# Attention in four placed chains behind the GLU, low passes first, ten weight buffers through the down projection, and ScalarE rows for the SSM's angles and decay

## The chip, the cores and the metric

The kernel runs on one core of a Trainium2 chip. The metric is the device time of one execution in microseconds (us), as the median of three runs. The engines named below are TensorE (PE in the profile, PEld for its weight loads), VectorE (DVE), ScalarE (ACT) and SyncE (SP, which issues the DMAs). The compiled program fixes an order of instructions on each engine; each engine then works through its own list in that order and stops at an instruction whose input or buffer is not there yet.

## The reference

One decoder block on 256 tokens of width 2048. The columns of one input projection feed a state-space model (SSM) with a gate (GLU) and a sparse attention; both halves go through one output projection, a normalisation, and a feed-forward part with a width-3 convolution.

```python
proj = h @ w_in[l]
u_ssm, q, k, v, qi, ki, wi = jnp.split(proj, split_at, axis=-1)
y_ssm = _s5_mixer(u_ssm, ...)      # a decaying, turning state per channel; then
                                   # y = gelu(y);  y * sigmoid(y @ w_glu + b_glu)
y_attn = _dsa_attention(q, k, v, qi, ki, wi * idx_w_scale)
                                   # relu(qi . ki), weighted sum over 16 index heads, causal,
                                   # the 64 best keys of each query, softmax with a slope per head
mix = jnp.concatenate([y_ssm, y_attn], axis=-1) @ w_out[l]
h = _layer_norm(DEEPNORM_ALPHA * h + mix, ln1_g[l], ln1_b[l])
f = (gelu(conv(h @ w_up)) * (h @ w_gate)) @ w_down      # 5632 wide, 44 tiles of 128
h = _layer_norm(DEEPNORM_ALPHA * h + f, ln2_g[l], ln2_b[l])
```

## The kernel before

All matrix products are made from a high and a low part of each operand: `mm3` issues three matmuls (high by high, low by high, high by low) for one product of 128 rows.

**Weights.** A table of sources (`order`) is cut into halves of 128x1024 numbers. `fetch` brings one half by DMA into a raw tile (SP), makes its high part on ACT (`wh`, L133) and its low part on DVE (`wl`, L136). `next_half` keeps `state["ahead"]` halves made in advance, four as a rule. Extra buffers for some halves come from the table `special`, at times and places where another tile's memory is free.

**Input projections** (`acc`, L186 to L188). The projections for the SSM, the index queries, keys, values and two groups of four query heads (`q0`, `q1`) run one after another, 16 products each. `pump` lets a background job issue a few instructions after each product. The SSM is such a job, in four rounds (`ssm_in`): each round makes angles (`angles`, L362), sines and cosines, the decay rows (L547) and a scan on DVE. Another is the indexer: matmuls (L655), `rel` on ACT (L661), weighted sums `score` on DVE (L666), eight rounds of taking and striking out the eight best (L671, L672), and a mask `nm` for each block `b` of 128 queries (L675).

**GLU and attention.** `glu_in` makes Gelu of the SSM's output and splits it. `attention(c)` does for one key head `c` block 0 and then block 1 of the queries: scores on PE (L720), mask added on DVE (L724), maximum (L726), four Exp on ACT, a reciprocal and four scalings on DVE (L734), transposes on PE (L740), a copy `pt` on ACT (L743), products with the values (L747) and a split into `mix`. It is a generator: each `yield` waits for the next `pump`. `attention(0)` is pumped beside the products of the GLU, `attention(1)` beside those of the output projection. `in_turn` ties each function that needs a table of ACT (Sin, Gelu, Exp, Sigmoid) behind the last such one in the order in which the program is written, so the Sigmoid of the first GLU tile is written behind the Exp of `attention(0)`.

**Output projection, feed-forward.** The output projection accumulates in column groups `db` of 512, units of two products (`rows_half`), for 128 tokens each. The feed-forward's up and gate products go tile by tile through `wide_half`, which issues eight high passes (512 columns) and eight low passes (256 columns) for each half `kh` of the 2048 rows; in the second half one high pass is put last. The down projection (`e`) takes two halves for each of 44 tiles `f`; its last five tiles (`LAG`) are run for 128 tokens first and for the other 128 afterwards, so that ten halves must be held at once, and `state["ahead"]` is raised from four to ten at `f` = 34.

## Time and profile before

| what | us |
|---|---|
| median of three runs | 1144.31 |
| the three runs | 1144.85, 1138.44, 1144.31 |
| the profiled execution, its time | 1139.62 |
| the profiled execution, its span | 1137.8 |
| PE busy in the span | 1097.6 (96%) |
| DVE busy | 748.2 (66%) |
| ACT busy | 563.7 (50%) |
| DMA, mean over the span | 180 GB/s |

The rows further down are of the profiled execution; times in them count from the start of its span, which is 1.8 us shorter than its time. A row's bracket, where it has one, gives the engine's idle time before it and what ended that. PEclk is the clock that TensorE was granted: 1.00 and 0.50 stand for 2.4 and 1.2 GHz.

### The profile page before, as it was taken

What the parts mean: (1) busy time and instruction counts of PE and PEld (TensorE: products, weight loads), DVE (VectorE), ACT (ScalarE), POOL (GpSimd) and SP (SyncE); (2) the same over time, 40 slices, a digit from 0 to 9 for tenths busy, and PEclk for the clock granted to TensorE, in tenths of its full rate; (3) what the DMA queues carried; (4) which work ended last, traced back from release to release, by engine and by line L of the source; (5) the groups of instructions that cost most, each with busy time, mean ns of one, the idle gap of its engine ahead of it and who ended that gap; (6) DMA issues with size and microseconds to landing.
All of it is one profiled execution on the core that took longest, in us unless ns stands there. A gap on an engine that the chain in (4) does not pass through costs nothing.

```text
span 1137.8 us, 16797 instructions
## 1 busy us (share of the span) xinstructions
PE 1097.6 (96%) x6576; PEld 945.3 (83%) x6576; DVE 748.2 (66%) x1052; ACT 563.7 (50%) x813; POOL 0.2 (0%) x4
## 2 busy tenths in 40 slices
PE   8999999877999999999999999999999999999975
PEld 7998999767878888888888888888888888888864
DVE  7979998785666756677666565666565544444557
ACT  5865436445554755555444555545555444444430
POOL 0000000000000000000000000000000000000000
PEclk9999999988999999999999999999999999999988
DMA  8753444323566375555755555555554655555632
GB/s 267 237 167 115 159 145 145 139 74 108 207 212 214 104 259 192 185 185 187 262 194 190 189 189 187 192 187 187 185 188 165 216 189 186 186 188 190 212 130 74
DMA packets 59310, 204.44 MB, mean 180 GB/s; under 512 B 7264, under 2 KB 10080, under 8 KB 58592
## 3 DMA queue, kind: packets, MB, share of 16 engines
q1 hardware_dynamic: 59232, 203.38, 52.8%
q8 instruction: 51, 0.84, 0.3%
q14 instruction: 27, 0.22, 0.1%
HBM read 200.20 MB, written 2.10 MB: 178 GB/s over the span
## 4 chain that ended last, share of the span: by engine, by line
PE 86%; DMA 6%; DVE 3%; ACT 2%; issue 1%; SPq 1%; DVEq 0%; ACTq 0%
PE pd L206 41%; PE e L186 6%; PE e L188 6%; PE e L187 6%; PE acc L188 4%; PE acc L186 4%; PE acc L187 4%; DMA raw<-in_w_down_dram 3%; PE o L188 3%; PE o L187 3%; PE o L186 3%; DMA raw<-in_w_in_dram 1%; PE misc L599 1%; PE bu L556 1%; DVE wl L136 1%
## 5 line engine op out<-in xcount | busy, mean ns | idle before, releaser
L136 DVE TENSOR_TENSOR wl<-raw,wh 128x1024 fp32r<-128x1024 f32 x333 | 406.8, 1223 | 309.9 <-ACT wh L133 308.5
L133 ACT ACTIVATE wh<-raw 128x1024 fp32r<-128x1024 f32 x333 | 352.1, 1058 | 339.4 <-PE pd L206 141.5
L206 PE MATMUL pd<-mix,wh 128*128 128x512 f32 x1344 | 337.7, 393 | 0.7 <-ACT gate L1005 0.7
L206 PEld LDWEIGHTS pd<-mix,wh 128*128 128x128 f32 x1344 | 241.5, 189 | 44.0 <-ACT gate L1005 1.1
L206 PEld LDWEIGHTS pd<-mix,wl 128*128 128x128 f32 x1344 | 183.3, 190 | 13.1
L206 PE MATMUL pd<-mix,wl 128*128 128x256 f32 x1344 | 187.4, 282 | 0.0
L186 PE MATMUL e<-wh,acth 128*128 128x512 f32 x304 | 120.6, 397 | 5.5 <-ACT wh L133 5.5
L187 PE MATMUL e<-wh,actl 128*128 128x512 f32 x304 | 120.3, 396 | 0.0
L188 PE MATMUL e<-wl,acth 128*128 128x512 f32 x304 | 119.6, 396 | 0.5 <-DVE wl L136 0.5
L186 PE MATMUL acc<-x,wh 128*128 128x256 f32 (+1 forms) x400 | 113.9, 285 | 1.4 <-ACT x L181 1.2
L187 PE MATMUL acc<-x,wl 128*128 128x256 f32 (+1 forms) x400 | 114.2, 286 | 0.7 <-DVE wl L136 0.5
L188 PE MATMUL acc<-x,wh 128*128 128x256 f32 (+1 forms) x400 | 114.1, 285 | 0.8 <-DVE x L182 0.8
L186 PEld LDWEIGHTS acc<-x,wh 128*128 128x128 f32 (+1 forms) x400 | 75.8, 190 | 3.1 <-ACT x L181 1.4
L187 PEld LDWEIGHTS acc<-x,wl 128*128 128x128 f32 (+1 forms) x400 | 75.8, 190 | 2.2 <-DVE wl L136 0.7
L188 PEld LDWEIGHTS acc<-x,wh 128*128 128x128 f32 (+1 forms) x400 | 75.9, 190 | 2.1 <-DVE x L182 1.0
L186 PEld LDWEIGHTS e<-wh,acth 128*128 128x128 f32 x304 | 57.1, 188 | 20.0 <-ACT wh L133 6.2
L188 PEld LDWEIGHTS e<-wl,acth 128*128 128x128 f32 x304 | 57.1, 188 | 15.0 <-DVE wl L136 1.0
L187 PEld LDWEIGHTS e<-wh,actl 128*128 128x128 f32 x304 | 57.1, 188 | 13.8
L175 ACT ACTIVATE hc<-hc 128x256 f32<-128x256 f32 x44 | 18.4, 417 | 69.8 <-DVE hc L1046 69.8
L1033 DVE TENSOR_TENSOR sum<-sum,pd 128x256 f32<-128x256 f32 x84 | 34.9, 415 | 0.0
L188 PE MATMUL o<-wl,mix 128*128 128x512 f32 x80 | 31.9, 398 | 0.0
L186 PE MATMUL o<-wh,mix 128*128 128x512 f32 x80 | 31.6, 397 | 0.0
(262 smaller groups left out, 1201.7 us busy)
## 6 DMA issues: line engine op xcount, KB each, us to landing
raw<-in_w_gate_dram SPq DMA_DIRECT2D x88, 512.0 KB, 4.1
raw<-in_w_up_dram SPq DMA_DIRECT2D x88, 512.0 KB, 4.1
raw<-in_w_down_dram SPq DMA_DIRECT2D x88, 512.0 KB, 3.7
raw<-in_w_in_dram SPq DMA_DIRECT2D x51, 512.0 KB, 4.1
raw<-in_w_out_dram SPq DMA_DIRECT2D x32, 512.0 KB, 4.6
raw<-in_w_glu_dram SPq DMA_DIRECT2D x8, 512.0 KB, 3.8
raw<-in_w_v_dram SPq DMA_DIRECT2D x4, 512.0 KB, 4.5
z<-in_x_n_dram SPq DMA_DIRECT2D x1, 2048.0 KB, 8.8
```

Of the source, the lines that this page charges most:

```text
L133: A.activation(h[:, :w], raw[:, :w], AF.Copy)
L136: V.tensor_sub(l[:, :w], raw[:, :w], h[:, :w].bitcast(F32))
L175: ins = A.activation(*args, **kw)
L186: T.matmul(out, lhsT=lh[0], rhs=rh[0], start=start, stop=False)
L187: T.matmul(out, lhsT=lh[1], rhs=rh[0], start=False, stop=False)
L188: return T.matmul(out, lhsT=lh[0], rhs=rh[1], start=False, stop=stop).ins
L206: ins = T.matmul(out[:, 0] if low else out, lhsT=w, rhs=r, start=kh == 0 and i == 0, stop=kh == 1 and i == 15)
L556: T.matmul(bu[:, sd, ri, k:k + 128], lhsT=bt[r, 2 * bi + c_, h, ri, :], rhs=ustk[r, c_, h, :], start=True, stop=True)
L599: T.matmul(yp[32 * q:32 * q + 32, c_, e, k1:], lhsT=cbd[k1 * 2 + ri][:, ct * 4 + q, :], rhs=hv[ri][:, q % 2, k:k + 128 - k1], start=False, ...
L1033: V.tensor_tensor(t, t, p[:, 0], op=ALU.add)
```

## The change

1. **Angles and decay rows.** The one DVE product of 128x1024 in `angles` and the one for `dec` become eight ACT products of 128x128 each (a copy with a scale from a column), in each of the four rounds of the SSM.
2. **Attention.** `attention(c)` becomes a class `Attend` with four steps (scores, weights, turn, values) and one object for each key head and block: `a00`, `a10` (block 0), `a01`, `a11` (block 1). The scores of `a00` and `a10` are issued behind GLU tiles 3 and 4, their weights behind the whole GLU; everything else is issued at numbered units of the output projection, and the order written there is kept by hand on PE.
3. **GLU.** It runs without a background job; its first two tiles are interleaved, six products of each, then the last two of each.
4. **Output projection.** Three column groups are accumulated at once, over the SSM's half of the rows first and the attention's afterwards; the order of its weights, the extra buffers and the reading ahead of ten follow that order.
5. **Low passes first.** In the second half of `wide_half` the eight low passes come ahead of the eight high ones.
6. **Down projection.** Extra buffers for the last 80 halves instead of the last 20, and `ahead` is ten from `f` = 4 on. The split activations of tiles 1 to 43 move into the memory of two `hl` tiles, four to a slot, used in turn.

```diff
-    order += [w_out_d[i] for i in (0, 1, 4, 5, 2, 3, 6, 7, 8, 9, 10, 11, 12, 13, 14, 15)]
+    order += [w_out_d[i] for i in (0, 1, 4, 5, 8, 9, 2, 6, 10, 3, 7, 11, 12, 13, 14, 15)]
...
-        steps = list(passes(0)) + list(passes(1))
-        if kh:
-            steps.append(steps.pop(7))
+        steps = list(passes(1)) + list(passes(0)) if kh else list(passes(0)) + list(passes(1))
...
+    def by_pair(out, a, bi, row):
+
+        for s_ in range(2):
+            for ch in range(4):
+                i = bi * 8 + ch * 2 + s_
+                A.activation(out[:, s_, ch * 128:(ch + 1) * 128], row, AF.Copy, scale=a[:, i:i + 1])
...
-        V.tensor_tensor(v4(c), by_pair(f2, bi), row(cc("iota")), op=ALU.mult)
+        by_pair(c, f2, bi, cc("iota"))
...
-        V.tensor_tensor(v4(dec), by_pair(r2, bi), row(cc("after0")), op=ALU.mult)
+        by_pair(dec, r2, bi, cc("after0"))
...
-    def beside_q():
-        yield from glu_in()
-        yield from attention(0)
-
-    add_bg(beside_q(), 1)
+    a00, a10, a01, a11 = (Attend(c, b) for b in range(2) for c in range(2))
...
+    add_bg(glu_in(), 1)
     qt += proj_four("q1")
     drain()
...
+    first_glu = [(glu_acc(nt), next_half()) for nt in range(2)]
+    for some in (range(6), range(6, 8)):
+        for acc, half in first_glu:
+            glu_products(acc, half, some)
+    for nt in range(8):
...
+        in_turn(sgm, acc[:, :S], AF.Sigmoid, bias=pc("bglu", nt))
+        V.tensor_tensor(sgm, sgm, yt[nt], op=ALU.mult)
+        split(h[:, nt % 4, :], l[:, nt % 4, :], sgm)
+        if nt == 3:
+            a00.scores()
+        if nt == 4:
+            a10.scores()
...
-    add_bg(attention(1), 2)
...
-    for db, some in ((0, range(4)), (1, range(4)), (0, range(4, 8)), (1, range(4, 8)), (2, range(8))):
...
+    a00.weights()
+    a10.weights()
+    beside = {2: a01.scores, 3: a01.weights, 6: a00.turn, 7: a10.turn, 9: a00.values, 10: a10.values,
+              11: a11.scores, 12: a11.weights, 14: a01.turn, 17: a01.values, 22: a11.turn, 25: a11.values}
+    unit = 0
+    with tc.manual_schedule(engines={mybir.EngineType.PE}):
+        for some in (range(4), range(4, 6), range(6, 8)):
...
+            for db in range(3):
+                for i in some:
+                    half = next_half()
+                    for b in range(2):
+                        beside.get(unit, lambda: None)()
+                        rows_half(oacc[db][b], mix, 2 * i, half, b, 16)
+                        unit += 1
...
-    for i in range(4 * LAG):
+    for i in range(16 * LAG):
         if i % (2 * LAG) < 2 * LAG - 4:
-            special[len(halves) - 4 * LAG + i] = spare2(i % (2 * LAG))
+            special[len(halves) - 16 * LAG + i] = spare2(i % (2 * LAG))
...
-        if f == NF - 2 * LAG:
+        if f == NF - 8 * LAG:
             state["ahead"] = 2 * LAG
```

Three places show what this does to the order on the engines.

On ACT, at the start of the input projections, before (L317 brings the SSM's input `u` out of PSUM, L590 makes a diagonal, L366 and L175 make the cosines):

```order
L133 ACTIVATE wh<-raw 128x1024
L317 ACTIVATE u_308<-acc 128x128x2
L133 ACTIVATE wh<-raw 128x1024
L590 ACTIVATE dd<-cst,prm 128x128
L317 ACTIVATE u_342<-acc 128x128x2
L133 ACTIVATE wh<-raw 128x1024
L317 ACTIVATE u_374<-bu 128x128x2
L133 ACTIVATE wh<-raw 128x1024
```

The same place now:

```order
L133 ACTIVATE wh<-raw 128x1024
L315 ACTIVATE u_308<-acc 128x128x2
L133 ACTIVATE wh<-raw 128x1024
L353 ACTIVATE cos_422<-cst,f_420 128x128 x8
L585 ACTIVATE dd<-cst,prm 128x128
L315 ACTIVATE u_342<-acc 128x128x2
L353 ACTIVATE dec<-cst,r_421 128x128 x7
L133 ACTIVATE wh<-raw 128x1024
L353 ACTIVATE dec<-cst,r_421 128x128
L315 ACTIVATE u_374<-bu 128x128x2
L133 ACTIVATE wh<-raw 128x1024
```

Sixteen ACT products of 128x128 now stand between the weight splits of the first round, fifteen of them ahead of one split.

On ACT, at the GLU, before (`e` are the attention's Exp, `sgm` the GLU's Sigmoid, `mix` the split results):

```order
L175 ACT_TABLE_LOAD
L175 ACTIVATE e_2639,sm<-e_2639,mx 128x128 x4
L133 ACTIVATE wh<-raw 128x1024 x2
L743 ACTIVATE pt<-misc 128x512
L133 ACTIVATE wh<-raw 128x1024
L181 ACTIVATE mixh<-misc 128x4x128
L175 ACTIVATE e_2715,sm<-e_2715,mx 128x256 x4
L175 ACT_TABLE_LOAD
L175 ACTIVATE sgm<-glu,prm 128x256 x2
```

The end of the GLU's part on ACT now:

```order
L175 ACTIVATE sgm<-glu,prm 128x256
L133 ACTIVATE wh<-raw 128x1024
L175 ACTIVATE sgm<-glu,prm 128x256
L175 ACT_TABLE_LOAD
L175 ACTIVATE e_3051,sm<-e_3051,mx 128x128 x3
L181 ACTIVATE mix_2904<-sgm 128x256
L175 ACTIVATE e_3051,sm<-e_3051,mx 128x128
L175 ACTIVATE e_3100,sm<-e_3100,mx 128x128 x4
L133 ACTIVATE wh<-raw 128x1024
L181 ACTIVATE mix_2904<-sgm 128x256
L133 ACTIVATE wh<-raw 128x1024
L175 ACTIVATE e_3288,sm<-e_3288,mx 128x256 x3
```

Sigmoid stood behind both blocks' Exp of `attention(0)`; now all Exp stand behind the eight Sigmoid, and the split of the last GLU tiles (`mix_2904`) stands between and behind the first Exp.

On PE, at the GLU, before (L740 are transposes of a block's weights, L747 the products with the values, L720 the scores of block 1):

```order
L188 MATMUL glu<-yl_2571,wh 128x256
L740 MATMUL misc<-cst,e_2639 128x128 x4
L747 MATMUL misc<-pt,kv 128x512
L720 MATMUL misc<-kv,q_2311 128x256 x4
L186 MATMUL glu<-yh_2568,wh 128x256
```

Steps `a00.turn` and `a10.turn` now (L739 are the transposes; `o_3234` and `o_3235` are the output projection's sums for the two token blocks):

```order
L188 MATMUL o_3235<-wl,mix_2904 128x512
L739 MATMUL misc<-cst,e_3051 128x128 x4
L186 MATMUL o_3234<-wh,mix_2904 128x512
L187 MATMUL o_3234<-wh,mix_2904 128x512
L188 MATMUL o_3234<-wl,mix_2904 128x512
L186 MATMUL o_3234<-wh,mix_2904 128x512
L187 MATMUL o_3234<-wh,mix_2904 128x512
L188 MATMUL o_3234<-wl,mix_2904 128x512
L739 MATMUL misc<-cst,e_3100 128x128 x4
L186 MATMUL o_3235<-wh,mix_2904 128x512
```

The steps of one attention chain followed each other directly on PE; now whole units of six output matmuls stand between them.

## Rows read from the trace of the kernel before

**Rows 1.** Windows: length, busy PE, PEld, DVE, ACT, POOL, clock, DMA share, GB/s.

```profile
7.40:218.60 211.20, 207.97 (x1997) 196.03 (x1996) 183.61 (x227) 116.75 (x169) 0.00 (x0) 1.00 0.53 176
218.60:278.20 59.60, 42.92 (x270) 36.98 (x269) 45.36 (x128) 30.51 (x65) 0.00 (x0) 0.83 0.18 62
...
401.00:1092.00 691.00, 690.51 (x3641) 590.73 (x3641) 407.59 (x521) 341.77 (x469) 0.00 (x0) 1.00 0.57 195
1092.00:1102.50 10.50, 4.48 (x12) 2.83 (x11) 5.56 (x5) 4.17 (x4) 0.00 (x0) 0.68 0.45 151
```

**Rows 2.** Waits of PE: who for whom, total us, times, longest us.

```profile
PE glu L186 <- ACT sgm L175: 9.9, 1, 9.9
PE e L186 <- ACT wh L133: 5.5, 2, 4.8
PE misc L655 <- ACT rel L661: 3.3, 3, 1.4
PE misc L720 <- DVE mixl L182: 2.0, 1, 2.0
```

**Rows 3.** Windows, columns as in Rows 1: stretches at the lower clock.

```profile
225.30:232.10 6.80, 6.20 (x24) 5.37 (x25) 6.66 (x27) 3.56 (x8) 0.00 (x0) 0.50 0.00 0
...
262.40:266.30 3.90, 3.84 (x18) 3.85 (x19) 3.16 (x8) 2.77 (x8) 0.00 (x0) 0.50 0.00 0
...
1099.50:1102.50 3.00, 2.92 (x7) 2.35 (x8) 2.45 (x2) 1.08 (x2) 0.00 (x0) 0.50 0.00 0
```

**Rows 4.** Timeline ahead of PE's longest wait: start, us, instruction, count, [idle before].

```profile
255.11 0.43 DVE L675 TENSOR_TENSOR nm<-nm,cst 128x256 f32<-128x256 f32 x1
255.64 1.42 DVE L724 SCALAR_TENSOR_TENSOR e<-misc,nm 128x256 f32<-128x256 f32 x4
258.54 0.51 ACT L175 ACTIVATE e<-e,mx 128x256 f32<-128x256 f32 x1 [9.37 <-DVE mx L727]
260.63 1.28 ACT L175 ACT_TABLE_LOAD   x1
```

**Rows 5.** Groups by form, 7.4 to 278.2 us: count, busy us, mean ns, idle before.

```profile
L547 DVE TENSOR_TENSOR dec<-r,cst 128x1024 f32<-128x1024 f32 x4 | 4.9, 1230 | 0.0
L590 ACT ACTIVATE dd<-cst,prm 128x128 f32<-128x128 f32 x8 | 3.2, 395 | 4.2 <-PE misc L593 4.2
L133 ACT ACTIVATE wh<-raw 128x1024 fp32r<-128x1024 f32 x66 | 69.6, 1058 | 53.8 <-DMA raw<-in_w_in_dram 26.5 <-PE acc L188 9.2 <-PE acc L187 7.3
```

**Rows 6.** Timeline of ACT, 28 to 36 us, where the first products will stand.

```profile
28.45 1.06 ACT L133 ACTIVATE wh<-raw 128x1024 fp32r<-128x1024 f32 x1 [0.87 <-DMA raw<-in_w_in_dram]
...
31.61 1.06 ACT L133 ACTIVATE wh<-raw 128x1024 fp32r<-128x1024 f32 x1 [1.29 <-DMA raw<-in_w_in_dram]
...
34.52 1.06 ACT L133 ACTIVATE wh<-raw 128x1024 fp32r<-128x1024 f32 x1 [1.30 <-DMA raw<-in_w_in_dram]
```

**Rows 7.** Timeline of PE in the up and gate products, two tiles' passes.

```profile
599.90 1.11 PE L206 MATMUL pd<-mix,wl 128*128 128x256 f32 x8
600.85 1.78 PE L206 MATMUL pd<-mix,wh 128*128 128x512 f32 x7
602.47 1.11 PE L206 MATMUL pd<-mix,wl 128*128 128x256 f32 x8
603.42 2.23 PE L206 MATMUL pd<-mix,wh 128*128 128x512 f32 x9
605.49 1.11 PE L206 MATMUL pd<-mix,wl 128*128 128x256 f32 x8
```

**Rows 8.** Timeline of DVE in the down projection, halves before and after reading ten ahead.

```profile
1046.46 1.23 DVE L136 TENSOR_TENSOR wl<-raw,wh 128x1024 fp32r<-128x1024 f32 x1 [1.57 <-ACT wh L133]
...
1049.26 1.23 DVE L136 TENSOR_TENSOR wl<-raw,wh 128x1024 fp32r<-128x1024 f32 x1 [1.24 <-ACT wh L133]
1052.41 1.23 DVE L136 TENSOR_TENSOR wx<-raw,wx 128x1024 fp32r<-128x1024 f32 x1 [1.92 <-ACT wx L133]
...
1091.44 1.22 DVE L136 TENSOR_TENSOR wxl<-raw,wxh 128x1024 fp32r<-128x1024 f32 x1
```

More of the change, by code (lines that the diff above doesn't have):

```diff
@@ L107, in block_kernel @@
     for n, src in enumerate(order):
-        if n == 41:
-            halves_before_db2 = len(halves)
+        if n == 42:
+            halves_before_spare = len(halves)
         w = src.shape[1]
@@ L704, in block_kernel, with __init__, scores @@
     post = pre.enter_context(pool("post"))
-    def attention(c):
-        qs = qt[4 * c:4 * c + 4]
-        for b in range(2):
-            w = 128 * (b + 1)
-            e4 = post.tile([P, 4, S], F32, name="e4", bufs=2)
-            mx = post.tile([P, 4], F32, name="mx", bufs=2)
-            sm = post.tile([P, 4], F32, name="sm", bufs=2)
+    class Attend:
+        def __init__(self, c, b):
+            self.c, self.b, self.w = c, b, 128 * (b + 1)
+        def scores(self):
+            c, b, w = self.c, self.b, self.w
+            self.e4 = e4 = post.tile([P, 4, w], F32, name=f"e4{b}", bufs=2)
+            self.mx = mx = post.tile([P, 4], F32, name="mx", bufs=4)
             nh = 512 // w
@@ L777, in block_kernel, with glu_products, glu_acc @@
     mix = [hl[0], hl[1], mix[2], hl[3]]
[L778 to L791 removed]
+    def glu_products(acc, half, kts):
+        for kt in kts:
+            mm3(acc[:, :S], (half[0][:, kt * P:(kt + 1) * P], half[1][:, kt * P:(kt + 1) * P]), (yh[kt], yl[kt]),
+                kt == 0, kt == 7)
+    def glu_acc(nt):
+        return pso.tile([P, 512], F32, name="glu", tag=("o00", "o01", "o10", "o11")[nt % 4])
+    first_glu = [(glu_acc(nt), next_half()) for nt in range(2)]
[3 more added lines that the diff above has]
+    for nt in range(8):
+        h, l = mix[nt // 4]
+        if nt < 2:
+            acc = first_glu[nt][0]
+        else:
+            acc = glu_acc(nt)
+            glu_products(acc, next_half(), range(8))
+        sgm = post.tile([P, S], F32, name="sgm", bufs=2)
+        in_turn(sgm, acc[:, :S], AF.Sigmoid, bias=pc("bglu", nt))
[5 more added lines that the diff above has]
+            a10.scores()
     tmp.close()
@@ L879, in parts @@
             if j:
-                t = post.tile([P, 4, 128], F32, name="h1f", bufs=2)
+                t = post.tile([P, 4, 128], F32, name="h1f", tag="pt", bufs=3)
                 for k in range(4):
@@ L894, in spare @@
                 lambda: proj.tile([P, 1024], F32R, name="wql", tag=("qi1", "q1")[n]))
-    first = halves_before_db2
-    for i in range(24):
+    first = halves_before_spare
+    for i in range(22):
         if i % 11 < 7:
             special[first + i] = spare(i)
-    oacc = {}
     def rows_half(out, tiles, kt0, half, b, n):
@@ L923, in block_kernel @@
                     nc.sync.dma_start(out=ln10[:, i], in_=ln_d[i:i + 1, :512].broadcast_to([P, 512]))
-        if db == 2:
-            state["ahead"] = 10
-        if some[0] == 0:
-            oacc[db] = row_banks(db % 2)
-        for i in some:
-            half = next_half()
-            for b in range(2):
-                rows_half(oacc[db][b], mix, 2 * i, half, b, 16)
-        if 7 in some:
-            for b in range(2):
-                residual(b, db, oacc[db][b])
+                state["ahead"] = 10
+            for db in range(3):
[5 more added lines that the diff above has]
+                        unit += 1
+                if 7 in some:
+                    for b in range(2):
+                        residual(b, db, oacc[db][b])
     oacc[3], gacc = row_banks(1), row_banks(0)
@@ L1008, in block_kernel @@
     pre.close()
+    wx2 = ctx.enter_context(pool("wx2"))
     ff = ctx.enter_context(pool("ff"))
```

80 lines of the change are left out of this document (32 added, 48 removed).

## The prediction

> **What bounds the kernel now.** I read the windows by stage first. PE is busy nearly throughout: from 401 to 1092 us it is idle for 0.49 of 691 us, from 7 to 219 us for 3.2 of 211 [rows 1]. The only large holes are 59.60 - 42.92 = 16.7 us between 218.6 and 278.2, and 10.50 - 4.48 = 6.0 us between 1092 and 1102.5, and both windows have a mean clock below 1 [rows 1]. So nearly all time is PE's own work, which this change does not shrink; what can be won lies in two places.
>
> The list of PE's waits says what ended the holes [rows 2]. The longest, 9.9 us, is the first matmul of a GLU tile waiting for a Sigmoid to empty its PSUM bank. Three waits, 3.3 us in all, are index products waiting for `rel`. The third kind, 2.0 us, are scores queued behind a split of `mix`. In the down projection 5.5 of the 6.0 us are waits for the high part of a half.
>
> The timeline ahead of the 9.9 us shows the chain [rows 4]: DVE finishes the mask of block 1 at 255.5, makes the scores, ACT begins Exp at 258.54 after 9.37 us of idleness, then loads a table for 1.28 us from 260.63, and only then comes the Sigmoid. GLU tiles were long done; the Sigmoid stood in ACT's order behind an Exp that hung on the top-64 search. The hole is an order, not work.
>
> Three stretches at clock 0.50, the 1.2 GHz level, come during or behind these holes [rows 3]. PE was busy there for 6.20, 3.84 and 2.92 us; half of each is what the full clock would have given back: 3.1, 1.9 and 1.5 us.
>
> **The GLU and attention.** The GLU no longer has attention between its products, Sigmoid no longer waits for Exp, and the index products lie among those of `q1`. In the order that is compiled, the last index product stands 88 projection matmuls ahead of the GLU. The search and masks stay on DVE's list ahead of the first product of a Sigmoid with `y`, but the only PE work that needs them is now scores at GLU tiles 3 and 4 or in the output projection. Cover for DVE: 45.36 us of work in the 59.6 us stage [rows 1], part of which (the scalings, the maxima) moves behind the GLU. What goes: 16.7 us of holes and 3.1 + 1.9 us at the lower clock, 21.7 us. If one wait like the 2.0 us row remains, that much less.
>
> **Attention at set places.** A unit of the output projection is half of what a half of the down projection takes, 2.80 us [rows 8], since it has six of the same twelve matmuls: 1.4 us. After the last Sigmoid ACT needs 1.28 us for a table, and at most 258.54 to 260.63, 2.1 us, for each four Exp [rows 4]: `a00` is through at 3.4, `a10` at 5.5, with a split among them 6; a DVE step as long as the 1.42 us of the scores puts them at 4.8 and 7.4. Their places, units 6 and 7, come at 8.4 and 9.8. The slack is 2.4 us or more. Tighter is unit 6's own input: the split of the last GLU tile stands behind eight Exp, a table and a weight split, and its low part behind scores on DVE, which I reckon to be ready about when unit 6 wants it; at unit 11 the second bank of `a11`'s scores waits for a split. Lower bound 0, upper bound three waits of the 2.0 us kind, 6 us; I take 2.
>
> **The down projection.** Before reading ahead, halves come one per 1049.26 - 1046.46 = 2.80 us, PE's pace. With ten ahead, 17 halves are split from 1052.41 to 1091.44, one per 39.03/16 = 2.44 us [rows 8]. So each half gains 0.36 us of lead. The last five tiles, run for half of the tokens first, want all ten halves at once, and what was missing is the 6.0 us. That takes 6.0/0.36 = 17 halves more; the change adds 60. Even the whole way from four ahead to ten, 6 x 2.80 = 17 us, takes 47. Gain 6.0 + 1.5 (clock) = 7.5 us; lower bound 0, if DMA does not keep the pace. DMA was busy for 0.57 of the time at PE's pace [rows 1], which leaves room. The splits of activations now wait for a slot of four tiles, freed four tiles (22 us) before.
>
> **Products on ACT.** Eight DVE instructions of 1.23 us go, 9.8 us; 64 on ACT of 0.395 us come, 25.3 us, going by the diagonal `dd`, the same operation and size [rows 5]. In the projections DVE is busy for 184 of 211 us and ACT for 117 [rows 1], so on average the move goes the right way. The price is at the start: sixteen products, 6.3 us, between splits that had 0.87 + 1.29 + 1.30 = 3.5 us of idleness ahead of them, waiting for DMA [rows 6]. The split behind them comes up to 2.9 us later, while DVE is relieved of 2.5 us. From this and the moves of other steps that go with it I take a loss of 3 us. Lower bound 0; upper bound 2.9 us in each of four rounds, 11.6 us, against which stand 53.8 us of idleness ahead of the splits [rows 5].
>
> A rule speaks against this edit. The Trainium skill, page ScalarE: Activation LUTs, section Rules for kernel authors, says to put multiplications on VectorE and not on ScalarE. The trace agrees as to the price (0.395 us eight times, 3.2 us, where DVE takes 1.23), and by the rule alone the 64 products would cost 25.3 - 9.8 = 15.5 us more engine time; nothing of the sum hangs on it, since PE is the bound and ACT has the idle time.
>
> **Low passes first.** Seven high passes take 602.47 - 600.85 = 1.62 us, nine take 605.49 - 603.42 = 2.07 [rows 7]: 0.225 each, with 0.045 us left over for a change of width there and back. The new order has one such pair fewer in each of 84 tiles, at most 3.8 us; eight low passes at 0.95 are no dearer than 8 x 0.119, so part of it may be rounding of two decimals. I take a gain of 1, bounds 0 and 3.8. That the low part is now wanted sooner costs nothing: PE waits 0.49 us in 691 [rows 1], and halves are made four ahead.
>
> The order of `w_out`, the buffers of the output projection, `h1f` in the memory of `pt` and the interleaved first tiles only rename or reorder; PE has work around each of them, and what a late one would cost is in the 6 us above.
>
> **Sum.** 1139.6 - 21.7 - 7.5 - 1 + 3 + 2 = 1114.4 against the profiled execution. The three runs lie 1.2 below and 4.7 and 5.2 above that execution, 2.9 on average: 1117.
>
> **Rivals.**
> (a) *All covered.* No new wait: 1139.6 - 29.2 - 1 + 2.9 = 1112. For it: ACT's idle time. Against: DVE's 87% in the projections.
> (b) *ACT's products delay the weights.* All four rounds lose 2.9 us and one stretch follows at the lower clock, as after other holes of 1 to 5 us (3.1 us): 11.6 + 3.1 instead of 3, so 1129. For it: the sixteen products in two of the first gaps. Against: later rounds stand where ACT waits for DMA and PE.
> (c) *Set places are too early.* PE's order is fixed by hand, so a late transpose stops the whole output projection: 6 us and two stretches of 3.1 us instead of 2, so 1127. For it: the split behind eight Exp. Against: 2.4 us slack at the nearest places.
> (d) *DMA gives no lead.* The 7.5 us stay: 1125. Against: 2.44 us per half shown before.
> (e) *Slower.* Each of the eight groups of products stands ahead of a split that PE needs at once: 3.2 us each, with 3.1 us at the lower clock each time, 50 us against 29.2 + 1 won, so 1139.6 + 20 + 2.9 = 1162. It turns slower than before from the fifth group on (5 x 6.3 = 31.5). Against: DVE's low part, not ACT, ended the one wait for a weight there; ACT is at 55% [rows 1]. This is what the rule above would come to here if ACT had no idle time: the Trainium skill, ScalarE: Activation LUTs, Rules for kernel authors.
>
> **How the numbers follow.** Chances: forecast 0.60, (a) 0.08, (b) 0.15, (c) 0.09, (d) 0.04, (e) 0.04. About 1% is what a measurement of this kernel can tell from no change, here 1133 to 1156. A quarter of (b) and a third of (c), with clocks falling more often, come to lie above 1133: 0.07 within. Slower is (e), 0.04. The rest, 0.89, is faster. The range 1107 to 1131 takes in the forecast's own bounds (loss 0 to 9 instead of 5), most of (b), (c) and (d), and leaves out (e), the ends of (b) and (c), and, for runs as low as the lowest of before, a part of (a), about 0.16.
>
> **What would show it.** Right: the GLU follows `q1` without holes and ends before 260 us (278.2 - 21.7 + 3) instead of 278.2; no table load between Exp and Sigmoid before the eighth Sigmoid; no stretch at 0.50 before the tail; ten halves ready by 1000 us and no wait at the start of the last five tiles. The early price shows as a wait of `acc` for `wh` or `wl` between 35 and 60 us, the places' price as waits of L739, L714 or `o` in the first 30 units. Wrong: waits of `acc` above 8 us in all, the clock at 0.50 in the output projection, or DVE's mask so late that the scores of `a00` at GLU tile 3 hold up the GLU.

## The result and the profile after

| what | before | after |
|---|---|---|
| median | 1142.52 (4 runs, 1138.44 to 1144.85) | 1109.19 (4 runs, 1108.72 to 1110.08) |
| the profiled execution | 1139.62 | 1110.08 |
| its span | 1137.8 | 1108.3 |

The ratio is 0.9713 [0.9681, 0.9745]: faster by 2.9%. The forecast was 1117, with a range of 1107 to 1131. The time lies in the range, 8 us below the forecast, and the stages show that it came out by terms that were off in both directions, so in part by luck.

Windows of after by stage: up to the GLU, the GLU, the output projection (in two pieces), the up and gate products, the down projection, the tail. Columns as in [rows 1]: stretch and length, busy time of PE, PEld, DVE, ACT and POOL with their counts, clock, DMA share, GB/s. The last two rows are two short stretches of the first.

```profile
7.40:237.00 229.60, 224.14 (x2034) 206.04 (x2035) 193.92 (x286) 142.05 (x252) 0.00 (x0) 0.99 0.49 160
237.00:261.90 24.90, 24.90 (x213) 24.90 (x213) 21.97 (x50) 14.52 (x23) 0.00 (x0) 1.00 0.52 172
261.90:340.00 78.10, 78.10 (x343) 62.03 (x342) 48.34 (x72) 44.37 (x75) 0.00 (x0) 1.00 0.61 210
340.00:388.40 48.40, 47.71 (x224) 38.52 (x222) 35.73 (x55) 28.48 (x49) 0.00 (x0) 1.00 0.51 182
388.40:857.20 468.80, 468.80 (x2697) 414.23 (x2698) 295.04 (x399) 243.20 (x348) 0.00 (x0) 1.00 0.59 195
857.10:1096.80 239.70, 239.66 (x1057) 198.00 (x1055) 134.16 (x158) 103.43 (x127) 0.00 (x0) 1.00 0.56 186
1096.80:1108.30 11.50, 0.00 (x0) 0.00 (x0) 7.63 (x17) 0.20 (x1) 0.00 (x0) 0.71 0.29 96
12.90:16.30 3.40, 3.40 (x18) 3.40 (x17) 2.85 (x8) 0.94 (x2) 0.00 (x0) 0.50 0.73 230
169.90:173.30 3.40, 3.40 (x17) 3.18 (x16) 3.40 (x4) 1.14 (x2) 0.00 (x0) 0.50 0.72 247
```

From 237 us to the tail PE is idle for less than 1 us. The holes of [rows 1] are gone, the one at the GLU and the one at the last five tiles. Two stretches at clock 0.50 (the 1.2 GHz level) stand in the projections, where before's execution has none. PE was busy through both of them, and half of that is lost: 1.7 us each. Like those of [rows 3] they stand behind waits of PE, here short ones (PE's timeline, after):

```profile
11.31 0.38 PE L186 MATMUL acc<-x,wh 128*128 128x256 f32 x1 [1.56 <-ACT x L181]
...
12.57 0.38 PE L188 MATMUL acc<-x,wh 128*128 128x256 f32 x1 [0.76 <-DVE x L182]
...
169.00 0.65 PE L186 MATMUL acc<-x,wh 128*128 128x256 f32 x2 [0.86 <-ACT kv L691]
```

The first stretch isn't the change's: four kernels further down that are the kernel before with a part of the change have it in their traces as well (`rows_alone`, `down_alone`, `glu_first`, `rows_glu`).

The span is 29.5 us shorter. The stages' boundaries, read from PE's instructions, split this up: before, the output projection ended at 401.5, the up and gate products at 871.8 and the down projection at 1126.3; after, at 388.4, 857.1 and 1096.8. To the end of the output projection that is 13.1 us, in the up and gate products 1.6, in the down projection 14.8. The GLU itself takes 24.6 us instead of 49.7. The output projection takes 126.0 instead of 122.6, since matmuls of the first key head's attention now stand in it.

PE's waits after, columns as in [rows 2]:

```profile
PE acc L186 <- ACT x L181: 1.6, 1, 1.6
...
PE acc L186 <- ACT kv L691: 0.9, 1, 0.9
PE acc L187 <- DVE wl L136: 0.8, 2, 0.5
PE acc L188 <- DVE x L182: 0.8, 1, 0.8
PE pd L204 <- ACT gate L1018: 0.7, 1, 0.7
```

All four rows of [rows 2] have gone: no Sigmoid, no high part of a half of the down projection, no `rel`, no split of `mix`. What is left is short and stands where one part begins, most of it in the input projections. No wait belongs to one of the set places of the attention.

### The profile page after: what moved, and what is told of

It is laid out like the page before. It is cut to its first block, busy times and chain, and to the rows that moved or that the text cites. A ratio compares the mean times of both kernels' runs of the same rounds, so it can differ in the third digit from the quotient of the medians.

```text
span 1108.3 us, 16859 instructions
## 1 busy us (share of the span) xinstructions
PE 1089.2 (98%) x6576; PEld 945.8 (85%) x6576; DVE 739.4 (67%) x1044; ACT 578.7 (52%) x876; POOL 0.2 (0%) x4
## 4 chain that ended last, share of the span: by engine, by line
PE 85%; DVE 6%; DMA 3%; ACT 2%; issue 2%; SPq 1%; DVEq 0%; ACTq 0%
PE pd L204 42%; PE e L186 7%; PE e L188 7%; PE e L187 7%; PE o L188 3%; PE o L186 3%; PE o L187 3%; PE acc L187 3%; PE acc L188 3%; PE acc L186 3%; DMA raw<-in_w_in_dram 2%; DVE wl L136 2%; PE misc L650 1%; SPq L530 1%; ACT wh L133 1%
## 5 line engine op out<-in xcount | busy, mean ns | idle before, releaser
L136 DVE TENSOR_TENSOR wl<-raw,wh 128x1024 fp32r<-128x1024 f32 x299 | 364.7, 1222 | 250.1 <-ACT wh L133 247.5
L133 ACT ACTIVATE wh<-raw 128x1024 fp32r<-128x1024 f32 x299 | 315.6, 1056 | 252.2 <-PE pd L204 138.5
L204 PE MATMUL pd<-mix,wh 128*128 128x512 f32 x1344 | 321.4, 391 | 0.7 <-ACT gate L1018 0.7
L204 PE MATMUL pd<-mix,wl 128*128 128x256 f32 x1344 | 174.8, 283 | 0.0
L136 DVE TENSOR_TENSOR wxl<-raw,wxh 128x1024 fp32r<-128x1024 f32 x42 | 51.4, 1225 | 44.6 <-ACT wxh L133 42.6
L133 ACT ACTIVATE wxh<-raw 128x1024 fp32r<-128x1024 f32 x42 | 44.6, 1061 | 55.9 <-DMA raw<-in_w_down_dram 24.2
L187 PE MATMUL e<-wh,acthl 128*128 128x512 f32 x152 | 59.1, 389 | 0.0
L186 PE MATMUL e<-wh,acthl 128*128 128x512 f32 x152 | 59.0, 389 | 0.0
L188 PE MATMUL e<-wl,acthl 128*128 128x512 f32 x152 | 58.3, 389 | 0.0
L175 ACT ACTIVATE hc<-hc 128x256 f32<-128x256 f32 x44 | 18.4, 417 | 76.4 <-DVE hc L1060 76.4
L186 PE MATMUL e<-wxh,acthl 128*128 128x512 f32 x128 | 49.8, 389 | 0.0
L187 PE MATMUL e<-wxh,acthl 128*128 128x512 f32 x128 | 49.8, 389 | 0.0
L188 PE MATMUL e<-wxl,acthl 128*128 128x512 f32 x128 | 49.8, 389 | 0.0
```

The lines of the kernel that those rows point to most:

```text
L133: A.activation(h[:, :w], raw[:, :w], AF.Copy)
L136: V.tensor_sub(l[:, :w], raw[:, :w], h[:, :w].bitcast(F32))
L175: ins = A.activation(*args, **kw)
L186: T.matmul(out, lhsT=lh[0], rhs=rh[0], start=start, stop=False)
L187: T.matmul(out, lhsT=lh[1], rhs=rh[0], start=False, stop=False)
L188: return T.matmul(out, lhsT=lh[0], rhs=rh[1], start=False, stop=stop).ins
```

## Theories

After the result I held three, each with a rival. **Down projection:** the 7 us beyond the forecast come from where the split activations now lie in SBUF; rival: from the longer lead or from the tiles' grouping. **Products on ACT:** they relieve DVE and gain time; rival: they cost the 3 us of the forecast and something else paid for it. **GLU and attention:** writing the GLU first takes the holes away by itself; rival: only together with the set places.

## Experiments on the down projection

In `e` the split activations are the stationary operand and the weights the moving one. PE's timeline shows the pace of products of one form, after and then before (start, us, instruction):

```profile
979.64 0.39 PE L186 MATMUL e<-wh,acthl 128*128 128x512 f32 x1
...
981.00 0.39 PE L186 MATMUL e<-wh,acthl 128*128 128x512 f32 x1
```

```profile
979.83 0.39 PE L187 MATMUL e<-wh,actl 128*128 128x512 f32 x1
...
981.23 0.39 PE L187 MATMUL e<-wh,actl 128*128 128x512 f32 x1
```

There are six products from the first to the second row: 1.36 us after, 1.40 before, and by the whole stage, without its holes and its time at the low clock, 227.0 against 233.9 ns. 1056 products x 6.9 ns = 7.3 us, and with the 6.0 us of holes and 1.5 us of clock this makes the 14.8.

**Activations as before, lead as after** (`high_acts`):

```diff
-    parts[slot] = ahl.tile([P, 4, 2, S], F32R, name="acthl", tag=f"hl{slot % 2}")
+    h = ff.tile([P, S], F32R, name="acth", bufs=LAG + 2)
+    l = ff.tile([P, S], F32R, name="actl", bufs=LAG + 2)
...
```

The extra halves' tiles (`wx`) are where they were before, and the pool `wx2` goes.

> The changed kernel, but in the down projection the split activations lie where they lay before: one tile each for the high and the low part, seven buffers, 152 to 166 KB into a partition, and the extra weight buffers as before too. Reading ten halves ahead from f = 4 stays. The down projection of the changed kernel took 239.7 us instead of 254.5, 14.8 less where 7.5 were forecast; its 1056 products start every 226.6 ns instead of 234. Place theory: the pace follows from where the split activations lie. Then the products go back to 233 or 234 ns, no wait returns, the down projection takes 246 to 247 us and the kernel 1109.2 + 6.9 = 1116. Lead theory: the pace comes with reading ahead, because less other work collides with the products. Then 227 ns stay and the time is 1109.

**Grouped tiles, but high in SBUF** (`high_group`):

```diff
...
-                parts[slot] = ahl.tile([P, 4, 2, S], F32R, name="acthl", tag=f"hl{slot % 2}")
+                parts[slot] = ff.tile([P, 4, 2, S], F32R, name="acthl", tag=f"ahi{slot % 2}")
```

Here too some of the extra halves' tiles move, into the place that the activations leave.

> The changed kernel, but the two tiles that hold four split activations each, high and low parts side by side, lie 171 to 187 KB into a partition instead of 68 to 84 KB. The grouping stays, the lead stays. Address theory: products whose stationary operand lies that high start every 232 to 234 ns; the down projection takes 246 us, the kernel 1116. Grouping theory: it is the high and low part lying side by side in one tile that makes 227 ns; then nothing changes, 239.7 us and 1109.

They took 1114.97 and 1115.07 us (one run each), where two kernels with the places of after took 1109.89 and 1109.07 on the same chip. Windows over the down projection, columns as above, of `high_acts` and of `high_group`:

```profile
856.00:1101.70 245.70, 245.68 (x1057) 197.82 (x1056) 132.72 (x153) 103.40 (x127) 0.00 (x0) 1.00 0.55 182
```

```profile
855.00:1101.00 246.00, 246.00 (x1056) 197.59 (x1055) 132.02 (x151) 102.81 (x125) 0.00 (x0) 1.00 0.55 181
```

PE is busy throughout at the full clock, nothing waits, and from its first to its last product the stage takes 245.6 and 246.5 us, 6 to 7 more. So the pace doesn't hang on the lead or on the grouping but on the place. The products with `wh`, which lies where it did, show it by themselves: they start every 226.7 ns in after and every 233.4 in both of these runs. So does tile 0 in after itself, whose activations stayed high (185 to 187 KB): its products at 857.09 and 858.49 us, six apart, lie 1.40 us apart as in the kernel before. By the addresses of the built programs (offset within a partition) the activations of tiles 1 to 43 lie at 68 to 84 KB in after, at 152 to 166 KB in `high_acts` and at 171 to 187 KB in `high_group`; `wh` lies at 35 to 52 KB in all of them. A third form came with `high_acts`: where its weights lie high too (`wxh`, 167 to 183 KB), most of the products take 227 to 229 ns, though the activations are high. So it isn't the place of one operand alone; that the two must lie on the same side fits these runs but is not shown (the last section has a pair that is slow with both high).

**The read-ahead raised later** (`late_lead`), which I took for the switch that makes the lead:

```diff
-        if f == NF - 8 * LAG:
+        if f == NF - 2 * LAG:
             state["ahead"] = 2 * LAG
```

> The changed kernel, but ahead is raised to ten only at f = 34, as before; the places of buffers and activations stay changed. Forecast's mechanism: the last five tiles wait again, about 6 us, and a stretch at 0.50 comes with it (1.5 us); at the faster pace of 227 ns a half is wanted every 2.72 us, so the lead grows by 0.28 instead of 0.36 us per half and the wait is rather 7 us: 1109.2 + 7 + 1.5 = 1118. If the pace comes with the lead, 234 ns return as well for the tiles up to f = 34, 5 us more: 1123. Rival, places alone suffice: 1109.

1109.89 us (one run) and no wait in the down projection: the expectation was missed. The instructions stand in the same order as in after, since the scheduler puts a fetch as early as a free buffer lets it. The next run took the buffers away as well.

**Extra buffers only for the last twenty halves** (`few_buffers`):

```diff
-    for i in range(16 * LAG):
+    for i in range(4 * LAG):
         if i % (2 * LAG) < 2 * LAG - 4:
-            special[len(halves) - 16 * LAG + i] = spare2(i % (2 * LAG))
+            special[len(halves) - 4 * LAG + i] = spare2(i % (2 * LAG))
...
```

The line of `late_lead` is in it too.

> The changed kernel, but only the last 20 halves have extra buffers, as before, and ahead is raised at f = 34; the places of the activations and of these buffers stay. Raising ahead late alone left every instruction in its order and changed nothing (1109.9), so it is the buffers that let splits run ahead. Buffer theory: the lead stays at 6 us until half 68 and grows from there by 2.72 - 2.44 us per half; the last five tiles wait again, 6 to 8 us, with 1.5 us at the lower clock: 1117 to 1119. The pace of 227 ns stays. Rival, the faster splits of the new places suffice: 1109.

1116.40 us (one run). Its longest wait, and below the window of the last five tiles, first of `few_buffers` and then of `late_lead`:

```profile
PE e L186 <- ACT wh L133: 4.3, 2, 2.6
```

```profile
1068.00:1079.00 11.00, 6.22 (x19) 4.12 (x19) 6.28 (x8) 5.09 (x6) 0.00 (x0) 0.74 0.56 185
```

```profile
1068.00:1079.00 11.00, 11.00 (x51) 9.09 (x50) 4.79 (x6) 1.06 (x1) 0.00 (x0) 1.00 0.00 1
```

The hole and the low clock of before are back, at the new pace: the stage takes 247.1 us, 7.4 more than after, where the forecast had priced them at 7.5. So the buffers make the lead: with them the later number changes nothing, without them the hole is back. The number raised early without the buffers was not run.

**The down projection's part alone**, on the kernel before (`down_alone`):

```diff
+    wx2 = ctx.enter_context(pool("wx2"))
-    for i in range(4 * LAG):
+    for i in range(16 * LAG):
...
```

The functions `act_split` and `spare2` and the line of `state["ahead"]` are as in the change.

> The kernel before with one part of the change: the buffers and places of the down projection. Theory from the runs so far: the wait at the last five tiles goes (6.0 + 1.5 us) and the products start every 227 instead of 234 ns (6.9 us): 14.4 us less than before, the down projection takes 239.7 instead of 254.5 us. Forecast's theory: 7.5 us less. Rival, it needs the rest of the change: less than 3.

1126.59 us (4 runs, 1124.48 to 1127.77), ratio 0.9889 [0.9862, 0.9916], 11.8 us below the 1138.43 of before beside it. Its window:

```profile
874.40:1114.10 239.70, 239.70 (x1057) 198.00 (x1055) 134.18 (x158) 103.40 (x127) 0.00 (x0) 1.00 0.57 186
```

The stage is after's to the tenth, 239.7. The whole time gains less than the stage's 14.8 us. The runs of before beside it lay between 1135.53 and 1141.48, and in the profiled execution the down projection starts at 874.4 us, in before's at 871.8: ahead of it, by half of PE's busy time at clock 0.50, an estimated 11.7 us were lost instead of 5.0. Why the clock was low for longer there stays open.

**The place in another stage** (`low_mix`): after, with the attention's first output moved from tiles at 132 KB or higher to one at 84 KB.

```diff
-    mix = [hl[0], hl[1], mix[2], hl[3]]
+    mix = hl
```

> The changed kernel with the first key head's attention output written straight into its hl tile, 84 KB into a partition, instead of into mixh and mixl at 132 to 140 KB. Address theory: products of the output projection with this operand as the stationary one and weights in the low tiles go from 232 to 227 ns; about 60 of them, 0.3 us; those with weights in the high tiles stay at 232 to 234 ns. The output projection takes 125.7 instead of 126.0 us; the kernel 1109, no difference that can be measured in the whole time. Rival, these products are slower for another reason: they stay at 232 ns.

Products of this operand with low weights took a median of 227 ns instead of 230 to 234. Over the output projection (window of `low_mix`) PE is busy for 125.33 us, in after for 126.01:

```profile
259.40:385.40 126.00, 125.33 (x566) 100.73 (x564) 84.38 (x127) 72.71 (x124) 0.00 (x0) 1.00 0.59 200
```

The whole time, 1110.78 (1107.16 to 1111.01, ratio 0.9753 [0.9725, 0.9781]), can't be told from after's. Products of this operand whose weights lie in spare tiles placed high stay at 231 to 233 ns: making one operand low doesn't help those.

## Experiments on the products on ACT

**Back to DVE, the rest as after** (`dve_rows`):

```diff
-                A.activation(out[:, s_, ch * 128:(ch + 1) * 128], row, AF.Copy, scale=a[:, i:i + 1])
...
+        V.tensor_tensor(out.rearrange("p s (c k) -> p s c k", c=4), v.unsqueeze(3).broadcast_to([P, 2, 4, 128]),
+                        row.unsqueeze(1).unsqueeze(1).broadcast_to([P, 2, 4, 128]), op=ALU.mult)
```

> The changed kernel with the angles' first products and the decay rows made on DVE again, one instruction of 128x1024 each; 64 instructions go from ACT, 8 come to DVE. Price theory: the sixteen products in the first gaps delay weights, waits between 35 and 60 us go (1 to 3 us): 1106 to 1108. Relief theory: DVE is the engine that is late in the projections, and 9.8 us more on it push the masks, the splits for the GLU and the products with y: 2 to 10 us more, 1111 to 1119. If neither, 1109.

1111.82 us (4 runs, 1109.54 to 1116.01), ratio 0.9783 [0.9748, 0.9818]: 2.6 above after's median, so the products on ACT are worth a gain and not the 3 us of loss that stand in the forecast. The gain is small beside the spread, and the lowest run lies among those of after; `rows_alone` below shows it clear of the noise. The profiled execution took 1116.01 us. Two of its waits, and two stretches that after doesn't have:

```profile
PE misc L648 <- ACT rel L654: 3.3, 3, 1.4
PE o L186 <- ACT sgm L175: 2.4, 1, 2.4
```

```profile
231.00:237.90 6.90, 6.55 (x25) 5.52 (x25) 6.76 (x28) 3.31 (x8) 0.00 (x0) 0.51 0.00 0
91.10:97.90 6.80, 6.80 (x29) 6.05 (x28) 6.80 (x7) 1.06 (x1) 0.00 (x0) 0.50 0.26 82
```

The first wait is the third row of [rows 2], with the same 3.3 us. With DVE doing the products, the rounds of the SSM end later, the index products are left over behind `q1`, and they wait for `rel` with nothing beside them; a stretch at the low clock follows (231.0). In after they lie among the products of `q1`. The stretch at 91.1 stands behind another wait, of 1.52 us for the DMA of `ustk`; `glu_first`, too, has such a wait and stretch there, `down_alone` the wait without the stretch, so it isn't counted for either theory. The price at the start that I looked for is there, but small (timeline of ACT, after):

```profile
29.46 2.45 ACT L353 ACTIVATE cos<-cst,f 128x128 f32<-128x128 f32 x8
32.53 2.11 ACT L353 ACTIVATE dec<-cst,r 128x128 f32<-128x128 f32 x7
34.54 1.04 ACT L133 ACTIVATE wh<-raw 128x1024 fp32r<-128x1024 f32 x1
```

Eight products take 2.45 us back to back, not the 3.2 that I took from the single duration. The split at 34.54 starts when it did before, at 34.52 [rows 6], and the two waits for `wl` in the time that I named are 0.35 and 0.46 us. The Trainium skill, page ScalarE: Activation LUTs, section Rules for kernel authors, says to put multiplications on VectorE. The prices agree with it (2.45 us for eight on ACT, 1.23 for the one instruction on DVE [rows 5]); the time went the other way, as DVE was the engine that came late.

**The products on ACT alone**, on the kernel before (`rows_alone`):

```diff
-        V.tensor_tensor(v4(c), by_pair(f2, bi), row(cc("iota")), op=ALU.mult)
+        by_pair(c, f2, bi, cc("iota"))
...
-        V.tensor_tensor(v4(dec), by_pair(r2, bi), row(cc("after0")), op=ALU.mult)
+        by_pair(dec, r2, bi, cc("after0"))
```

Here `by_pair` issues eight `A.activation`, as in the change.

> The kernel before with one part of the change: the angles' first products and the decay rows on ACT. In its order the last index product stands 88 products ahead of the GLU, as in the changed kernel; without this part it stands among the products of the GLU in both kernels. Relief theory: DVE, relieved of 9.8 us and with the SSM issued earlier, finishes the masks earlier: the 3.3 us of index waits and one stretch at 0.50 go, and the 9.9 us hole ahead of the Sigmoid shrinks by the 15 to 20 us by which the mask comes earlier, so to nearly nothing: 10 to 17 us less than before. Forecast's theory: these products cost about 3 us in the first gaps and win nothing by themselves: 0 to 3 us more than before.

1130.75 us (6 runs, 1127.81 to 1134.36), ratio 0.9928 [0.9904, 0.9951]: 7.7 us gained by this edit alone, where the theory had expected 10 to 17. Its longest wait and the one stretch at the low clock near the GLU:

```profile
PE glu L186 <- ACT sgm L175: 4.9, 1, 4.9
```

```profile
251.60:258.40 6.80, 4.25 (x20) 4.25 (x21) 4.49 (x14) 5.25 (x13) 0.00 (x0) 0.50 0.30 104
```

No index product waits any more, and the wait for the Sigmoid has fallen from 9.9 to 4.9 us, though Sigmoid still stands behind Exp: the search that Exp hangs on is through earlier. So half of the 9.9 us, which the forecast put down to the order of GLU and attention, is had by this edit too, and the 3.3 us for `rel` with the stretch behind them (3.1) by this edit and not by that order: `dve_rows`, which has the order, still waits for them. The profiled execution took 1127.81 us, 11.8 less than before's: 8.1 of them lie ahead of the down projection and 3.7 in it, where the wait for a high part is 2.4 us instead of 5.5 [rows 2]; why that is so these runs leave open.

## Experiments on the GLU and the set places

**GLU first, on the kernel before** (`glu_first`): both heads' attention pumped beside the output projection.

```diff
-        yield from attention(0)
...
-    add_bg(attention(1), 2)
+    def both():
+        yield from attention(0)
+        yield from attention(1)
+    add_bg(both(), 1)
```

> The kernel before, with one part of the change in a plain form: the GLU runs without attention(0) beside it, and attention(0) and attention(1) are pumped one after the other beside the output projection. Order theory: the holes of the GLU (9.9 + 2.0 + 0.7 + 0.7 us) and 1.9 us at the lower clock go, the 3.3 us of the index products stay: about 15 us less than before. The rest of the middle gain would then come from the earlier SSM and index. Rival, placing is what counts: the attention's waits move into the output projection, 4 to 8 us of them, and 8 to 11 us are left.

1134.0 us (11 runs, 1132.93 to 1140.72), ratio 0.9963 [0.9944, 0.9982]. The profiled execution took 1140.72 us, so its stages don't add up to the gain of the median, 4.2 us. The GLU takes 28.0 us instead of 49.7, but the output projection 139.2 instead of 122.6, where after, with the same matmuls in it, takes 126.0. Its waits:

```profile
PE misc L740 <- DVE e L734: 3.3, 1, 3.3
PE misc L655 <- ACT rel L661: 3.3, 3, 1.4
...
PE o L186 <- ACT mix L181: 1.6, 2, 1.0
...
PE o L186 <- ACT sgm L175: 1.3, 1, 1.3
PE misc L747 <- ACT pt L743: 1.2, 2, 0.6
```

The expected 15 us did not come: part of the hole moved on. PE is idle for 8.0 us of these 139.2 and loses an estimated 1.4 at clock 0.50; in before's 122.6 it is idle for 0.65. Transposes wait for the scaled rows, products with the values for the copy, the projection for late splits.

**Both, GLU first and the products on ACT** (`rows_glu`), with the attention still pumped:

```diff
-        V.tensor_tensor(v4(c), by_pair(f2, bi), row(cc("iota")), op=ALU.mult)
+        by_pair(c, f2, bi, cc("iota"))
...
+    add_bg(both(), 1)
```

> The kernel before with two parts of the change: the products on ACT, and the GLU without attention beside it, attention(0) and attention(1) pumped one after the other beside the output projection in its old column order. The places that the change sets by hand are left out. GLU first alone gained 4 us, because 9.2 us of waits came up in the output projection; the products alone gained 8. Place theory: the waits of the output projection stay (about 8 to 10 us, transposes waiting for scaled weights), since a generator issues each chain's steps one after another; the kernel ends 10 to 14 us below before, and the set places are worth the remaining 6 to 8 us. Relief theory: with the masks early the chains have time and the waits shrink to 3 us or less; then 18 us or more below before, and the places are worth little.

1135.08 us (8 runs, 1131.53 to 1137.19), ratio 0.9968 [0.9953, 0.9982]: worse than the products on ACT alone, and less than either theory had. The waits are those of the place theory, but DVE's relief brings nothing in time once the attention is pumped into the output projection, which takes 141.1 us:

```profile
PE misc L737 <- DVE e L731: 3.3, 1, 3.3
...
PE o L186 <- ACT mix L181: 1.9, 2, 1.3
```

So GLU first gains 4.2 us alone and loses 5 beside the products on ACT (2.9 instead of 7.7), as long as the attention's steps come when the pump reaches them. An estimate from these runs: 1138 less 2.9 for `rows_glu`, 11.8 for `down_alone` and 1.6 for the passes is 1122, and after takes 1109. The rest, about 12 us, is what the set places are worth with the edits that go with them. One of these is a rival: with three column groups at once 24 units, not 16, stand ahead of the first that needs the attention's output. No run has the one without the other, so how much is due to the places themselves is not shown.

**The places earlier** (`early_turn`): the two turns three units ahead, `a01` behind them.

```diff
-    beside = {2: a01.scores, 3: a01.weights, 6: a00.turn, 7: a10.turn, ...
+    beside = {3: a00.turn, 4: a10.turn, 5: a01.scores, 6: a01.weights, ...
```

> The changed kernel with the transposes of a00 and a10 at units 3 and 4 of the output projection instead of 6 and 7, and the scores and weights of a01 at units 5 and 6 instead of 2 and 3. In the changed kernel the weights of a00 are ready at 268.2 us and those of a10 at 272.0, PE takes them at 271.6 and 273.4. Place theory: PE reaches unit 3 at about 265.9 and unit 4 at 267.3 plus the wait, so it waits about 2 us for each, less what DVE gains by doing the scalings ahead of the scores of a01: 2 to 4 us in all, and perhaps one stretch at 0.50 (up to 3 us): 1111 to 1116. Rival, the scheduler's order on DVE and ACT follows the places and nothing waits: 1109.

1108.37 us (one run). One wait, and a window over its output projection:

```profile
PE misc L739 <- DVE e L732: 1.2, 1, 1.2
```

```profile
258.50:386.70 128.20, 126.29 (x566) 100.83 (x564) 85.22 (x127) 72.88 (x124) 0.00 (x0) 1.00 0.58 197
```

Up to the first up product that is 1.5 us more than after's 126.7, less than expected, and the whole time shows nothing of it. After's own timeline (DVE and PE) shows the slack at the places that were kept:

```profile
267.37 0.87 DVE L732 TENSOR_SCALAR e<-e,rs 128x128 f32<-128x128 f32 x4
271.20 0.87 DVE L732 TENSOR_SCALAR e<-e,rs 128x128 f32<-128x128 f32 x4
...
271.61 0.60 PE L739 MATMUL misc<-cst,e 128*128 128x128 f32 x4
...
273.44 0.60 PE L739 MATMUL misc<-cst,e 128*128 128x128 f32 x4
```

The first turn comes 271.61 - 268.24 = 3.4 us after its scaled rows, the second 273.44 - 272.07 = 1.4. I had reckoned 2.4 or more for both. Three units are 4.2 us; that the transposes waited only 1.2 fits the rival of this run in part, DVE's order following the places.

## Experiment on the order of passes

**The old order** (`old_passes`):

```diff
-        steps = list(passes(1)) + list(passes(0)) if kh else list(passes(0)) + list(passes(1))
+        steps = list(passes(0)) + list(passes(1))
+        if kh:
+            steps.append(steps.pop(7))
```

> The changed kernel with the old order of passes in the up and gate products: in the second half eight high passes with one of them put last, instead of low first. Width theory: a change of width there and back costs 19 ns for each of 84 tiles, 1.6 us: the up and gate stage takes 470.4 instead of 468.8 us and the kernel 1110.8. Rival: the stage is shorter for another reason, it stays at 468.8 us, 1109.2.

1109.07 us (one run). Window over the up and gate products, against 468.80 in after:

```profile
385.80:856.20 470.40, 470.38 (x2697) 413.93 (x2698) 295.33 (x399) 243.52 (x348) 0.00 (x0) 1.00 0.60 194
```

1.6 us longer, 19 ns for each of the 84 tiles, by the width theory. The whole time isn't longer: in this execution both low stretches of the projections, worth 1.7 us each, didn't come.

## Why the prediction came out right

| step | forecast | measured |
|---|---|---|
| holes and clock at GLU and attention | -21.7 | -21.7 |
| products on ACT, price | +3 | 0; by `dve_rows` a gain, in the row above |
| attention at set places | +2 | 0 |
| not in the sum, ahead of the feed-forward | 0 | +8.6 |
| low passes first | -1 | -1.6 |
| down projection, holes and clock | -7.5 | -7.5 |
| down projection, pace of products | 0 | -7.3 |

The forecast's rows add up to -25.2 us against the profiled execution, the measured ones to -29.5: that is 4.3 of the 8 us by which it was too high. The rest is the 2.9 us that it added because the runs of before lay above their profiled one; after's median lies 0.9 below its own.

**Up to the end of the output projection** the forecast was -16.7 and the trace shows -13.1. The holes went as reckoned, though part of them by another edit than the forecast named (next paragraph). What came instead is not any of the rivals: 3.4 us of low clock in two stretches of the projections, 2.2 us net of short waits where parts start, and 3.0 us that I can't assign row by row. The stretch at 12.9 is an accident of the execution, as said. Some of the last may be in the index products, which now lie in groups of four among others (PE's timeline, after):

```profile
208.59 0.28 PE L186 MATMUL acc<-x,wh 128*128 128x256 f32 x1
208.80 1.13 PE L650 MATMUL misc<-ki,qi 64*128 64x256 f32 x4
209.86 0.39 PE L187 MATMUL acc<-x,wl 128*128 128x256 f32 x1
210.18 1.13 PE L650 MATMUL misc<-ki,qi 64*128 64x256 f32 x4
```

A product of the projection takes 0.32 us between two groups of 64 rows (209.86 to 210.18), where it takes 0.12 among its own kind.

**Products on ACT** is the step with the wrong sign. "I take a loss of 3 us" came from the gaps at the start; DVE's 87% in the projections [rows 1] was quoted only for the average. It was the reason for the index products' lateness: `dve_rows` and `rows_alone` show that relief as a gain, and that 3.3 + 3.1 of the 21.7 us hang on it and not on the order of GLU and attention, to which the forecast gave them all. The first row of the table fits only because the change has both edits. What it brings and what the order brings overlap, so the parts' gains can't be added: each of them alone, on the kernel before, brings 7.7 (`rows_alone`), 4.2 (`glu_first`) and 11.8 (`down_alone`).

**The set places** cost nothing: the slack was 3.4 and 1.4 us instead of 2.4 or more, enough in both cases. "GLU first", a step that the forecast counted as free, isn't free without them: `glu_first` and `rows_glu` show 8.0 and 7.8 us of PE's idle time in the output projection. That the places alone cure it, and not the three column groups at once, is argued and not shown.

**The low passes** were worth 1.6, by a change of width of 19 ns where the rounded rows [rows 7] had allowed up to 45; `old_passes` shows the whole difference of the stage.

**The down projection's** holes and clock were right to the tenth, by their working too: from the low part's end to its first use the lead grows from 10.4 us at the 24th half to 21.4 at the 56th, 0.34 us per half (forecast 0.36). The last half is made while the last five tiles already run:

```profile
1069.40 0.39 PE L186 MATMUL e<-wx,acthl 128*128 128x512 f32 x1
...
1070.47 1.23 DVE L136 TENSOR_TENSOR wl<-raw,wh 128x1024 fp32r<-128x1024 f32 x1 [1.50 <-ACT wh L133]
```

The mis-sized term is in the sentence that the splits of activations "now wait for a slot of four tiles": it asked when the slot comes free and not where it lies. The move into another tile's memory gained 7.3 us, as much as the holes of that stage, and the forecast had it at nothing.

**Of the signs** that were to show it: the GLU ended at 261.9, not before 260, as it began later by what came on top in the projections. No stretch at 0.50 before the tail was wrong, twice. The full lead of ten halves was there at about 1006, not 1000. No table load between Exp and Sigmoid, no wait at the last five tiles, and waits of `acc` below 8 us were right.

## What to carry to other kernels

Work moved to an engine with idle time is priced not only where it arrives but also where it leaves: look which waits end on the engine that is relieved. Taking a chain out of one stage can move its wait into the next, as it did here while its steps followed each other at once; look how far apart their places are before counting the step as free. When tiles change memory, compare the pace of the products that read them, not only the times when they come free.

## What was not expected of the hardware

A 128x512 product of these parts starts every 226 to 228 ns when its stationary and its moving operand both lie in the lower part of the SBUF partition (stationary 64 to 100 KB, moving 32 to 134 KB), and every 230 to 235 ns with the stationary operand at 132 KB or higher and the moving one low; the other way round it is 231 to 238. With both high it is mostly 227 to 230 in the down projection (before's `wxh`, `high_acts`), but 230 to 233 for 36 products of the output projection. Left out of these figures are the products right behind a change of width: in the up and gate products of after the first five behind a narrower one start every 228 to 236 ns, with both operands low. Where the boundary lies (for the stationary operand between 100 and 132 KB, by these figures) and what makes it, these runs leave open. A stage with everything high was not tried.

The same short waits of PE were followed by the low clock in some executions and not in others. In after 3.4 us at 0.50 stand at 12.9 us behind waits of 1.56 and 0.76 us; `early_turn` has such a stretch behind 0.88 and 0.76, while `low_mix` kept the full clock behind 1.40 and 0.76 and before behind 1.24 and 0.76. At 169.9 us they stand behind waits of 0.20 and 0.86 us; `old_passes` has the same two waits and kept the full clock. So neither the length of the wait nor the change decides it alone; what does stays open.
